# Gate and up products of two SwiGLU layers: from token-major 512-column products to feature-major 256-column products

## The chip, the cores and the metric

The kernel runs on one core of a Trainium2 chip. The metric is the device time of one execution in microseconds. One core holds TensorE (matrix products, PE in the rows, with its weight loads shown apart as PEld), VectorE (DVE), ScalarE (ACT), GpSimd (POOL) and SyncE (SP), which here issues the weight transfers.

## What is computed

Two layers of a streaming encoder on 256 tokens of width 2048. Layer 0 mixes tokens with RWKV-7 heads and state-space heads, layer 1 with chunked attention; each layer ends with a dense SwiGLU block of 5632 hidden features. All of it is in float32. The block is the part that the change touches:

```python
def rms_norm(x, g):
    y = xf * lax.rsqrt(jnp.mean(xf * xf, axis=-1, keepdims=True) + NORM_EPS)
    return (y * g.astype(jnp.float32)).astype(x.dtype)

def swiglu(h, w_gate, w_up, w_down):
    return (jax.nn.silu(h @ w_gate) * (h @ w_up)) @ w_down

for l in range(DEPTH):
    ...                                    # token mixer, sandwich-normed
    h = rms_norm(x, norm_g[l, 2])
    x = x + rms_norm(swiglu(h, ffn_w_gate[l], ffn_w_up[l], ffn_w_down[l]), norm_g[l, 3])
```

## The kernel before, in words

Weights are too large for the core's memory and pass through it once. `stream` (L214) loads two 128-row pieces of a 512-column chunk at a time on SP's queue, and splits each piece into a rounded part `hi` (ScalarE, L230) and the rest `lo` (VectorE, L231), both in the type float32r; five tiles of each are in turn. A product in nearly full float32 precision is then three float32r products: x_hi with w_hi, x_hi with w_lo, x_lo with w_hi. `mm_chunk` (L235) makes them: for each of the nk row pieces and each half of the tokens (t = 0, 1) the activations [128 rows, 128 tokens] are the stationary operand, loaded anew for every product, and 512 weight columns are the moving one (L250, L251, L252). So a row piece takes six products of 512 columns, and the result is token-major: two PSUM tiles of 128 tokens x 512 features. Four PSUM tiles (pool `pmm`) let two chunks overlap.

The row scale of the norm (`rs`, one number per token) is not put on the activations. It is put on the results, where a token is a partition and the scale is one number per partition.

`ffn` (L338) runs for each layer over 11 groups j of 512 hidden features. A group is a gate chunk and an up chunk of 16 row pieces each: 2 x 16 x 6 = 192 products. ScalarE takes SiLU of the scaled gate out of PSUM (L347, two tiles), VectorE multiplies the scaled up result onto it (L350, two tiles). The down product needs hidden features on partitions, so TensorE transposes the group in eight 128 x 128 pieces (L359, into the pool `psa`), and ScalarE and VectorE split what comes out into `hh` (L360) and `hl` (L361). After the eleven groups `out_norm` (L300) runs the down product through `mm_chunk`, squares its result for the second norm (L317), multiplies by the norm's weights (L320 and L328) and adds the residual (L323).

In the built program, TensorE's stream has these transposes a few products into the next group, behind the first row piece's products; VectorE's stream has the two L350 four `lo` tiles into the next chunk.

Of the kernel before, what the change touches and what calls it, by code (L numbers as in the profile page):

```python
# [16 lines left out]
P = 128  # L17
T = 256
# [121 lines left out]
def encoder_body(ctx: ExitStack, tc: tile.TileContext, A):  # L140
# [73 lines left out]
    def stream(wname, n, nk, tail=None):  # L214
        """Yields the k-tiles of column chunk n, split: (hi, lo) tiles [P, 512]; tail: pool of the last four."""
# [19 lines left out]
    def mm_chunk(wname, n, st, width=512, tail=None):  # L235
        """st: list of (hi, lo) tiles [P, 4, T]; returns two PSUM tiles (tokens 0..127, 128..255)."""
# [27 lines left out]
    def split_evac(ps, sh, sl, kts, g):  # L264
        """ps [P, 2, T] (feature-major) times the feature column g(kt), split into hi and lo."""
# [7 lines left out]
    def pre_norm(xt, gname, tag):  # L273
        """xt: 4 token-major tiles [P, 2, 512]. Returns split x*g, feature-major, and its row scale."""
# [25 lines left out]
    def out_norm(ctx2, wname, st, grow, xres, tag, last=False):  # L300
        """x + rms_norm(st @ w) * g; returns 4 token-major tiles."""
# [4 lines left out]
        mg = []  # L306
        for n in range(4):
# [6 lines left out]
            with tc.high_priority(offset=PRI_NORM):  # L314
                for t in range(2):
                    junk = sm.tile([P, 512], mybir.dt.bfloat16, tag="junk", name=f"junk_{tag}_{n}_{t}", bufs=1)
                    act.activation(junk, ps[t], AF.Square, accum_out=ssq[:, t, n:n + 1])  # L317
                    if n == 3:
                        act.activation(rs[:, t:t + 1], ssq[:, t, 3:4], AF.Sqrt, scale=1.0 / D, bias=part[:, t:t + 1])
                        dve.tensor_tensor(m[:, t, :], ps[t], gb, op=ALU.mult)  # L320
# [6 lines left out]
                    else:  # L327
                        dve.tensor_tensor(m[:, t, :], ps[t], gb, op=ALU.mult)  # L328
# [9 lines left out]
    def ffn(l, xt):  # L338
        st, rs = pre_norm(xt, f"g{l}2", f"f{l}")
        with ExitStack() as mx:  # L340
            hp = mx.enter_context(tc.tile_pool(name=f"ff{l}", bufs=2 * NFF, reuse_waits="tile"))
            hid = []
            for j in range(NFF):
                pg = mm_chunk(f"w_gu{l}", 2 * j, st)
                sg = hp.tile([P, 2, 512], F32, tag="sg", name=f"sg_{l}_{j}", bufs=2)
                for t in range(2):
                    act.activation(sg[:, t, :], pg[t], AF.Silu, scale=rs[:, t:t + 1])  # L347
                pu = mm_chunk(f"w_gu{l}", 2 * j + 1, st)
                for t in range(2):
                    dve.scalar_tensor_tensor(sg[:, t, :], pu[t], rs[:, t:t + 1], sg[:, t, :],  # L350
                                             op0=ALU.mult, op1=ALU.mult)
                sh = hp.tile([P, 4, T], F32R, tag="hid", name=f"hh_{l}_{j}")
                sl = hp.tile([P, 4, T], F32R, tag="hid", name=f"hl_{l}_{j}")
                for hh in range(2):
                    ps = psa.tile([P, 2, T], F32, tag="sa", name=f"ht_{l}_{j}_{hh}")
                    for i in range(2):
                        for t in range(2):
                            c0 = (2 * hh + i) * P
                            pe.transpose(ps[:, i, t * P:(t + 1) * P], sg[:, t, c0:c0 + P], ident)  # L359
                    act.copy(sh[:, 2 * hh:2 * hh + 2, :], ps)  # L360
                    dve.tensor_tensor(sl[:, 2 * hh:2 * hh + 2, :], ps, sh[:, 2 * hh:2 * hh + 2, :].bitcast(F32),  # L361
                                      op=ALU.subtract)
                hid.append((sh, sl))
            return out_norm(mx, f"w_dn{l}", hid, 2 * l + 1, xt, f"fo{l}", last=l == 1)

# [561 lines left out]
```

## Time and profile before

| what | us |
|---|---|
| median of 3 runs | 2416.78 (2416.41 to 2418.41) |
| span of the profiled execution, first to last instruction | 2412.1 |
| TensorE busy in it | 2372.9 (98%) |
| weight loads of TensorE busy in it | 1940.9 (80%) |
| VectorE busy | 1424.3 (59%) |
| ScalarE busy | 1267.4 (53%) |
| DMA, mean of the span | 178 GB/s |

The profile was taken in an execution of its own, whose own time is shown only by its span. TensorE's products are pipelined, so the busy time of one (0.39 us) is longer than the distance from one start to the next; the distance is what a product costs in a stream.

### The profile page before, as it was taken

To read this page: it belongs to the slowest core of one execution; us is meant where nothing else is said; L and a number is where in the kernel's file an instruction comes from. 1 tells how busy PE (TensorE), PEld (TensorE's weight loads), DVE (VectorE), ACT (ScalarE), POOL (GpSimd) and SP (SyncE) were. 2 spreads that over 40 slices of the span, in tenths; PEclk is the share of its full clock that TensorE was granted. 3 is DMA by queue.
4 is the path that set the end of the run, shared out by engine and by line. 5 is a ranking of instruction groups with operands and counts; after the bars stand their busy time and mean duration, and the time that the engine had idled before them with its cause. 6 is when DMAs were issued, how large, how long until landed. Compare 5 with 4: busy or idle time off the path is not lost.

```text
span 2412.1 us, 31517 instructions
## 1 busy us (share of the span) xinstructions
PE 2372.9 (98%) x11374; PEld 1940.9 (80%) x11374; DVE 1424.3 (59%) x2340; ACT 1267.4 (53%) x2232; POOL 33.2 (1%) x60
## 2 busy tenths in 40 slices
PE   8999999999999999999999999999999999999998
PEld 7777778878888888888877888887888888888887
DVE  5865967665555555555556555556555555555554
ACT  6646545656445445444446555555544544544443
POOL 0000000000000000000000000000000000000000
PEclk9999999999999999999999999999999999999999
DMA  7433424656666666666675555565666666666665
GB/s 229 142 113 112 140 88 132 190 181 189 192 185 191 192 185 191 192 187 196 196 229 153 180 178 160 172 191 172 189 189 189 190 189 191 189 188 193 199 197 158
DMA packets 119358, 429.17 MB, mean 178 GB/s; under 512 B 13409, under 2 KB 13665, under 8 KB 119201
## 3 DMA queue, kind: packets, MB, share of 16 engines
q1 hardware_dynamic: 115424, 415.46, 56.6%
q0 software_dynamic: 2400, 9.18, 1.5%
q10 hardware_dynamic: 1376, 2.52, 0.3%
q8 instruction: 89, 1.46, 0.3%
q14 instruction: 69, 0.56, 0.1%
HBM read 425.01 MB, written 2.10 MB: 177 GB/s over the span
## 4 chain that ended last, share of the span: by engine, by line
PE 94%; DVE 4%; ACT 1%; issue 1%; DMA 1%; SPq 0%; POOL 0%; DVEq 0%; ACTq 0%; POOLq 0%
PE mm_w_gu L250 13%; PE mm_w_gu L252 13%; PE mm_w_gu L251 13%; PE mm_w_dn L251 7%; PE mm_w_dn L252 7%; PE mm_w_dn L250 7%; PE mm_w_qkv L250 4%; PE mm_w_qkv L251 4%; PE mm_w_qkv L252 4%; PE mm_w_in L252 3%; PE mm_w_in L251 3%; PE mm_w_in L250 3%; PE mm_w_oc L252 1%; PE mm_w_oc L251 1%; PE mm_w_oab L251 1%; PE mm_w_oab L252 1%
## 5 line engine op out<-in xcount | busy, mean ns | idle before, releaser
L231 DVE TENSOR_TENSOR lo_w_gu<-raw_w_gu,hi_w_gu 128x512 fp32r<-128x512 f32 x704 | 486.7, 692 | 433.3 <-ACT hi_w_gu L230 432.4
L230 ACT CAST hi_w_gu<-raw_w_gu 128x512 fp32r<-128x512 f32 x704 | 438.3, 623 | 473.4 <-DVE lo_w_gu L231 424.9
L250 PE MATMUL mm_w_gu<-hi_w_gu,sh_f 128*128 128x512 f32 x1408 | 551.3, 392 | 0.7 <-ACT sh_f L268 0.7
L251 PE MATMUL mm_w_gu<-lo_w_gu,sh_f 128*128 128x512 f32 x1408 | 551.3, 392 | 0.0
L252 PE MATMUL mm_w_gu<-hi_w_gu,sl_f 128*128 128x512 f32 x1408 | 549.2, 390 | 0.0
L231 DVE TENSOR_TENSOR lo_w_dn<-raw_w_dn,hi_w_dn 128x512 fp32r<-128x512 f32 x352 | 242.4, 692 | 218.5 <-ACT hi_w_dn L230 218.2
L230 ACT CAST hi_w_dn<-raw_w_dn 128x512 fp32r<-128x512 f32 x352 | 217.2, 621 | 246.5 <-DVE lo_w_dn L231 233.1
L250 PEld LDWEIGHTS mm_w_gu<-hi_w_gu,sh_f 128*128 128x128 f32 x1408 | 265.1, 188 | 55.6 <-ACT sh_f L268 1.2
L252 PEld LDWEIGHTS mm_w_gu<-hi_w_gu,sl_f 128*128 128x128 f32 x1408 | 265.0, 188 | 54.2
L251 PEld LDWEIGHTS mm_w_gu<-lo_w_gu,sh_f 128*128 128x128 f32 x1408 | 265.2, 188 | 53.2
L251 PE MATMUL mm_w_dn<-lo_w_dn,hh 128*128 128x512 f32 x704 | 276.8, 393 | 0.0
L252 PE MATMUL mm_w_dn<-hi_w_dn,hl 128*128 128x512 f32 x704 | 275.3, 391 | 0.0
L250 PE MATMUL mm_w_dn<-hi_w_dn,hh 128*128 128x512 f32 x704 | 274.8, 390 | 0.0
L231 DVE TENSOR_TENSOR lo_w_qkv<-raw_w_qkv,hi_w_qkv 128x512 fp32r<-128x512 f32 x192 | 132.5, 692 | 102.9 <-ACT hi_w_qkv L230 102.6
L230 ACT CAST hi_w_qkv<-raw_w_qkv 128x512 fp32r<-128x512 f32 x192 | 118.9, 621 | 108.6 <-DVE lo_w_qkv L231 65.5
L231 DVE TENSOR_TENSOR lo_w_in<-raw_w_in,hi_w_in 128x512 fp32r<-128x512 f32 x184 | 125.0, 689 | 56.1 <-ACT hi_w_in L230 54.9
L250 PEld LDWEIGHTS mm_w_dn<-hi_w_dn,hh 128*128 128x128 f32 x704 | 132.1, 188 | 30.1
L250 PE MATMUL mm_w_in<-hi_w_in,sh_in 128*128 128x512 f32 (+1 forms) x384 | 154.5, 402 | 1.4 <-ACT hi_w_in L230 1.4
L252 PE MATMUL mm_w_in<-hi_w_in,sl_in 128*128 128x512 f32 (+1 forms) x384 | 155.2, 404 | 0.0
L251 PEld LDWEIGHTS mm_w_dn<-lo_w_dn,hh 128*128 128x128 f32 x704 | 132.3, 188 | 28.4
L251 PE MATMUL mm_w_qkv<-lo_w_qkv,sh_qkv 128*128 128x512 f32 x384 | 155.1, 404 | 0.0
L252 PEld LDWEIGHTS mm_w_dn<-hi_w_dn,hl 128*128 128x128 f32 x704 | 132.2, 188 | 27.8
(335 smaller groups left out, 2837.5 us busy)
## 6 DMA issues: line engine op xcount, KB each, us to landing
raw_w_gu<-in_w_gu SPq DMA_DIRECT2D x352, 512.0 KB, 3.6
raw_w_dn<-in_w_dn SPq DMA_DIRECT2D x176, 512.0 KB, 4.2
raw_w_qkv<-in_w_qkv SPq DMA_DIRECT2D x96, 512.0 KB, 3.6
raw_w_in<-in_w_in SPq DMA_DIRECT2D x92, 512.0 KB, 3.6
raw_w_oab<-in_w_oab SPq DMA_DIRECT2D x32, 512.0 KB, 3.7
raw_w_oc<-in_w_oc SPq DMA_DIRECT2D x32, 512.0 KB, 4.2
bias<-in_bias POOLq DMA_DIRECT2D x4, 768.0 KB, 7.5
x_in<-in_x SPq DMA_DIRECT2D x4, 512.0 KB, 10.3
```

The lines of the kernel that those rows point to most:

```text
L230: act.copy(hi, raw[:, h, :])
L231: dve.tensor_tensor(lo, raw[:, h, :], hi.bitcast(F32), op=ALU.subtract)
L250: pe.matmul(o, lhsT=xh, rhs=h_[:, :width], start=k_ == 0, stop=False)
L251: pe.matmul(o, lhsT=xh, rhs=l_[:, :width], start=False, stop=False)
L252: pe.matmul(o, lhsT=xl, rhs=h_[:, :width], start=False, stop=k_ == nk - 1)
```

## The change

The gate and up products turn their operands round. A new `mm_feature` loads 128 x 128 pieces of the weights as the stationary operand and moves all 256 tokens past them. Its result has features on partitions and tokens in columns, as the down product wants it, and the eight transposes of a group go. A row piece is now four 128-feature pieces times three products, twelve products of 256 columns, each with its weight load. Since a token is now a column, the row scale of the gate is a multiplication by a tile `rb` that holds the 256 scales in every partition: `token_rows` makes it once per layer, with a product of ones and a diagonal matrix. SiLU then runs in place on the SBUF tile. The up result isn't scaled; its scale moves behind the down product, into `out_norm` (argument `rin`).

```diff
-                pg = mm_chunk(f"w_gu{l}", 2 * j, st)
-                sg = hp.tile([P, 2, 512], F32, tag="sg", name=f"sg_{l}_{j}", bufs=2)
-                for t in range(2):
-                    act.activation(sg[:, t, :], pg[t], AF.Silu, scale=rs[:, t:t + 1])
-                pu = mm_chunk(f"w_gu{l}", 2 * j + 1, st)
-                for t in range(2):
-                    dve.scalar_tensor_tensor(sg[:, t, :], pu[t], rs[:, t:t + 1], sg[:, t, :],
-                                             op0=ALU.mult, op1=ALU.mult)
+                pg = mm_feature(f"w_gu{l}", 2 * j, st)
+                if rb is None:
+                    rb = token_rows(hp, rs, f"f{l}")[:, None, :].broadcast_to([P, 2, T])
+                sg = hp.tile([P, 4, T], F32, tag="sg", name=f"sg_{l}_{j}", bufs=2)
+                for b in range(2):
+                    s2 = sg[:, 2 * b:2 * b + 2, :]
+                    dve.tensor_tensor(s2, pg[b], rb, op=ALU.mult)
+                    act.activation(s2, s2, AF.Silu)
+                pu = mm_feature(f"w_gu{l}", 2 * j + 1, st)
                 sh = hp.tile([P, 4, T], F32R, tag="hid", name=f"hh_{l}_{j}")
                 sl = hp.tile([P, 4, T], F32R, tag="hid", name=f"hl_{l}_{j}")
-                for hh in range(2):
-                    ps = psa.tile([P, 2, T], F32, tag="sa", name=f"ht_{l}_{j}_{hh}")
-                    for i in range(2):
-                        for t in range(2):
-                            c0 = (2 * hh + i) * P
-                            pe.transpose(ps[:, i, t * P:(t + 1) * P], sg[:, t, c0:c0 + P], ident)
-                    act.copy(sh[:, 2 * hh:2 * hh + 2, :], ps)
-                    dve.tensor_tensor(sl[:, 2 * hh:2 * hh + 2, :], ps, sh[:, 2 * hh:2 * hh + 2, :].bitcast(F32),
-                                      op=ALU.subtract)
+                for b in range(2):
+                    f2 = slice(2 * b, 2 * b + 2)
+                    dve.tensor_tensor(sg[:, f2, :], pu[b], sg[:, f2, :], op=ALU.mult)
+                    act.copy(sh[:, f2, :], sg[:, f2, :])
+                    dve.tensor_tensor(sl[:, f2, :], sg[:, f2, :], sh[:, f2, :].bitcast(F32), op=ALU.subtract)
...
+    def mm_feature(wname, n, st):
+        nk = 4 * len(st)
+        ps = [pmm.tile([P, 2, T], F32, tag="mm", name=f"mf_{wname}_{n}_{b}") for b in range(2)]
+        for kt, (hi, lo) in enumerate(stream(wname, n, nk)):
+            sh, sl = st[kt // 4]
+            xh, xl = sh[:, kt % 4, :], sl[:, kt % 4, :]
+            for b in range(2):
+                for i in range(2):
+                    f = slice((2 * b + i) * P, (2 * b + i + 1) * P)
+                    o = ps[b][:, i, :]
+                    pe.matmul(o, lhsT=hi[:, f], rhs=xh, start=kt == 0 and i == 0, stop=False, skip_group_check=True)
+                    pe.matmul(o, lhsT=hi[:, f], rhs=xl, start=False, stop=False, skip_group_check=True)
+                    pe.matmul(o, lhsT=lo[:, f], rhs=xh, start=False, stop=kt == nk - 1, skip_group_check=True)
+        return ps
...
+    def token_rows(pool_, rs, tag):
+        scr = pool_.tile([P, 4, T], F32, tag="sg", name=f"rsd_{tag}", bufs=2)
+        ones = scr[:, 0, 0:P]
+        pool.memset(ones, 1.0)
+        dg = scr[:, 1, :].rearrange("p (t j) -> p t j", t=2)
+        ps = psa.tile([P, 2, P], F32, tag="sa", name=f"rsb_{tag}")
+        for t in range(2):
+            dve.tensor_scalar(dg[:, t, :], ident, rs[:, t:t + 1], None, op0=ALU.mult)
+        pe.matmul(ps, lhsT=ones, rhs=dg, start=True, stop=True)
+        rb = pool_.tile([P, T], F32, tag="rsb", name=f"rb_{tag}", bufs=1)
+        act.copy(rb, ps.rearrange("p a b -> p (a b)"))
+        return rb
...
-                    act.activation(junk, ps[t], AF.Square, accum_out=ssq[:, t, n:n + 1])
+                    ri = 1.0 if rin is None else rin[:, t:t + 1]
+                    act.activation(junk, ps[t], AF.Square, scale=ri, accum_out=ssq[:, t, n:n + 1])
...
-                        dve.tensor_tensor(m[:, t, :], ps[t], gb, op=ALU.mult)
+                        scaled(m[:, t, :], ps[t], ri, gb)
```

`scaled` multiplies by `gb` as before, or, with `rin`, by the row scale and `gb` in one instruction.

TensorE, before, where the second group of layer 0 begins: `mm_w_gu_2_0` and `mm_w_gu_2_1` are the two token halves of that group's gate, `ht` the transposes of the group that has just ended.

```order
L250 MATMUL mm_w_gu_2_0_5323<-hi_w_gu_2_0_0_5327,sh_f_0_4840 128x512
L251 MATMUL mm_w_gu_2_0_5323<-lo_w_gu_2_0_0_5328,sh_f_0_4840 128x512
L252 MATMUL mm_w_gu_2_0_5323<-hi_w_gu_2_0_0_5327,sl_f_0_4841 128x512
L250 MATMUL mm_w_gu_2_1_5324<-hi_w_gu_2_0_0_5327,sh_f_0_4840 128x512
L359 MATMUL ht_0_0_5309<-cc,sg_0_5124 128x128
L359 MATMUL ht_0_1_5316<-cc,sg_0_5124 128x128
L251 MATMUL mm_w_gu_2_1_5324<-lo_w_gu_2_0_0_5328,sh_f_0_4840 128x512
L252 MATMUL mm_w_gu_2_1_5324<-hi_w_gu_2_0_0_5327,sl_f_0_4841 128x512
L359 MATMUL ht_0_0_5309<-cc,sg_0_5124 128x128 x3
L359 MATMUL ht_0_1_5316<-cc,sg_0_5124 128x128 x3
L250 MATMUL mm_w_gu_2_0_5323<-hi_w_gu_2_0_1_5331,sh_f_0_4840 128x512
```

TensorE, after, where the first gate chunk of layer 0 ends and the up chunk begins (the lines are those of the changed file; `mf_w_gu_0_1` holds features 256 to 511 of the gate chunk, `rsb` is the product that spreads the row scale).

```order
L357 MATMUL mf_w_gu_0_1_4947<-sh_f_3_4900,hi_w_gu_0_7_1_5192 128x256
L358 MATMUL mf_w_gu_0_1_4947<-sl_f_3_4901,hi_w_gu_0_7_1_5192 128x256
L359 MATMUL mf_w_gu_0_1_4947<-sh_f_3_4900,lo_w_gu_0_7_1_5193 128x256
L371 MATMUL rsb_f_5222<-rsd_f_5220 128x256
L357 MATMUL mf_w_gu_1_0_5233<-sh_f_0_4840,hi_w_gu_1_0_0_5237 128x256
L358 MATMUL mf_w_gu_1_0_5233<-sl_f_0_4841,hi_w_gu_1_0_0_5237 128x256
L359 MATMUL mf_w_gu_1_0_5233<-sh_f_0_4840,lo_w_gu_1_0_0_5238 128x256
```

Nothing but products of the chunks stands on TensorE between one group and the next now, save one `rsb` in each layer.

VectorE, before, around the end of the second group's up chunk (`mm_w_gu_3`):

```order
L231 TENSOR_TENSOR lo_w_gu_4_1_1_5731<-raw_w_gu_4_1_5724,hi_w_gu_4_1_1_5730 128x512
L350 SCALAR_TENSOR_TENSOR sg_1_5501<-mm_w_gu_3_0_5504,rs_pre,sg_1_5501 128x512
L350 SCALAR_TENSOR_TENSOR sg_1_5501<-mm_w_gu_3_1_5505,rs_pre,sg_1_5501 128x512
L231 TENSOR_TENSOR lo_w_gu_4_2_0_5749<-raw_w_gu_4_2_5746,hi_w_gu_4_2_0_5748 128x512
L231 TENSOR_TENSOR lo_w_gu_4_2_1_5753<-raw_w_gu_4_2_5746,hi_w_gu_4_2_1_5752 128x512
L361 TENSOR_TENSOR hl_1_5685<-ht_1_0_5686,hh_1_5684 128x512
```

VectorE, after, around the end of the second group's gate chunk (`mf_w_gu_2`), where before no VectorE instruction read PSUM:

```order
L231 TENSOR_TENSOR lo_w_gu_3_1_1_5837<-raw_w_gu_3_1_5830,hi_w_gu_3_1_1_5836 128x512
L389 TENSOR_TENSOR sg_1_5789<-mf_w_gu_2_0_5515,rb_f_5226 128x512
L389 TENSOR_TENSOR sg_1_5789<-mf_w_gu_2_1_5516,rb_f_5226 128x512
L231 TENSOR_TENSOR lo_w_gu_3_2_0_5867<-raw_w_gu_3_2_5864,hi_w_gu_3_2_0_5866 128x512
L231 TENSOR_TENSOR lo_w_gu_3_2_1_5871<-raw_w_gu_3_2_5864,hi_w_gu_3_2_1_5870 128x512
```

The two new L389 stand behind the first four `lo` tiles of the next chunk, at the place that L350 has at the end of an up chunk.

## Rows read from the trace of the kernel before

**Rows 1.** The page: busy time by engine, granted clock, chain that ended last.

```profile
PE 2372.9 (98%) x11374; PEld 1940.9 (80%) x11374; DVE 1424.3 (59%) x2340; ACT 1267.4 (53%) x2232; POOL 33.2 (1%) x60
...
PEclk9999999999999999999999999999999999999999
...
PE 94%; DVE 4%; ACT 1%; issue 1%; DMA 1%; SPq 0%; POOL 0%; DVEq 0%; ACTq 0%; POOLq 0%
```

**Rows 2.** Windows, 600 to 1000 us: length, then busy us (and instructions) by engine, clock, DMA.

```profile
600.00:1000.00 400.00, 400.00 (x1799) 329.88 (x1798) 220.99 (x324) 199.33 (x324) 0.00 (x0) 1.00 0.63 189
```

**Rows 3.** Timeline, gate/up stretch: start us, duration us, engine, line, names, shapes.

```profile
899.74 0.39 PE L251 MATMUL mm_w_gu<-lo_w_gu,sh_f 128*128 128x512 f32 x1
899.97 0.39 PE L252 MATMUL mm_w_gu<-hi_w_gu,sl_f 128*128 128x512 f32 x1
899.97 0.19 PEld L250 LDWEIGHTS mm_w_gu<-hi_w_gu,sh_f 128*128 128x128 f32 x1
900.20 0.39 PE L250 MATMUL mm_w_gu<-hi_w_gu,sh_f 128*128 128x512 f32 x1
...
910.62 0.39 PE L251 MATMUL mm_w_gu<-lo_w_gu,sh_f 128*128 128x512 f32 x1
```

**Rows 4.** Timeline, in-projection of layer 0, products of 464 columns, first and last.

```profile
29.79 0.37 PE L250 MATMUL mm_w_in<-hi_w_in,sh_in 128*128 128x464 f32 x1
...
39.60 0.37 PE L252 MATMUL mm_w_in<-hi_w_in,sl_in 128*128 128x464 f32 x1
```

**Rows 5.** Timeline, down product of layer 0, two L250 fifteen products apart.

```profile
1127.82 0.39 PE L250 MATMUL mm_w_dn<-hi_w_dn,hh 128*128 128x512 f32 x1
...
1131.26 0.39 PE L250 MATMUL mm_w_dn<-hi_w_dn,hh 128*128 128x512 f32 x1
```

**Rows 6.** The chain that ended last, in order of time: transposes of consecutive groups.

```profile
667.64 0.66 PE ht L359 x6
712.14 0.66 PE ht L359 x6
756.64 0.66 PE ht L359 x6
```

**Rows 7.** Timeline around the transposes of the first group of layer 0.

```profile
577.74 0.43 PE L359 MATMUL ht<-cc,sg 128*128 128x128 f32 x2
577.90 0.19 PEld L251 LDWEIGHTS mm_w_gu<-lo_w_gu,sh_f 128*128 128x128 f32 x1
...
578.01 0.19 PEld L252 LDWEIGHTS mm_w_gu<-hi_w_gu,sl_f 128*128 128x128 f32 x1
```

**Rows 8.** Timeline, plain float32 products of layer 0 (weight loads, then 256 moving columns).

```profile
354.96 1.86 PEld L789 LDWEIGHTS yd<-xc,L 128*128 128x128 f32 x16
...
210.22 1.89 PE L702 MATMUL g<-sgc,g 128*128 128x256 f32 x8
```

**Rows 9.** Groups by form: count, busy us, mean ns, then idle before and its releaser.

```profile
L231 DVE TENSOR_TENSOR lo_w_gu<-raw_w_gu,hi_w_gu 128x512 fp32r<-128x512 f32 x704 | 486.7, 692 | 433.3 <-ACT hi_w_gu L230 432.4
L350 DVE SCALAR_TENSOR_TENSOR sg<-mm_w_gu,rs_pre,sg 128x512 f32<-128x512 f32 x44 | 30.9, 742 | 0.0
L361 DVE TENSOR_TENSOR hl<-ht,hh 128x512 fp32r<-128x512 f32 x44 | 28.2, 682 | 0.0
L550 DVE TENSOR_TENSOR AA<-aa,cc 128x512 f32<-128x512 f32 x16 | 10.4, 685 | 2.1 <-PE aa L547 2.1
L347 ACT ACTIVATE sg<-mm_w_gu,rs_pre 128x512 f32<-128x512 f32 x44 | 30.2, 687 | 1.2
L360 ACT CAST hh<-ht 128x512 fp32r<-128x512 f32 x44 | 23.5, 585 | 0.0
```

More of the change, by code (lines that the diff above doesn't have):

```diff
@@ L298, in pre_norm, with out_norm @@
         return st, rsqrt_mean(ssum, D, EPS, "pre", [P, 2])
-    def out_norm(ctx2, wname, st, grow, xres, tag, last=False):
+    def out_norm(ctx2, wname, st, grow, xres, tag, last=False, rin=None):
         E = ctx2.enter_context(tc.tile_pool(name="E" + tag, bufs=4, reuse_waits="tile"))
@@ L306, in out_norm, with scaled @@
         mg = []
+        def scaled(out, p_, ri, gb_):
+            if rin is None:
+                dve.tensor_tensor(out, p_, gb_, op=ALU.mult)
+            else:
+                dve.scalar_tensor_tensor(out, p_, ri, gb_, op0=ALU.mult, op1=ALU.mult)
         for n in range(4):
@@ L327, in out_norm @@
                     else:
-                        dve.tensor_tensor(m[:, t, :], ps[t], gb, op=ALU.mult)
+                        scaled(m[:, t, :], ps[t], ri, gb)
                 if n == 0:
@@ L342, in ffn @@
             hid = []
+            rb = None
             for j in range(NFF):
-                pg = mm_chunk(f"w_gu{l}", 2 * j, st)
-                sg = hp.tile([P, 2, 512], F32, tag="sg", name=f"sg_{l}_{j}", bufs=2)
-                for t in range(2):
-                    act.activation(sg[:, t, :], pg[t], AF.Silu, scale=rs[:, t:t + 1])
-                pu = mm_chunk(f"w_gu{l}", 2 * j + 1, st)
-                for t in range(2):
-                    dve.scalar_tensor_tensor(sg[:, t, :], pu[t], rs[:, t:t + 1], sg[:, t, :],
-                                             op0=ALU.mult, op1=ALU.mult)
+                pg = mm_feature(f"w_gu{l}", 2 * j, st)
[7 more added lines that the diff above has]
+                pu = mm_feature(f"w_gu{l}", 2 * j + 1, st)
@@ L363, in ffn @@
                 hid.append((sh, sl))
-            return out_norm(mx, f"w_dn{l}", hid, 2 * l + 1, xt, f"fo{l}", last=l == 1)
+            return out_norm(mx, f"w_dn{l}", hid, 2 * l + 1, xt, f"fo{l}", last=l == 1, rin=rs)
     def mixer0(xt):
```

## The prediction

> **What bounds the kernel now.** I read the page first: TensorE is busy for 98% of the span, the chain that ended last runs through it for 94%, and the granted clock stands in the top tenth throughout [rows 1]. In a stretch that is gate/up work alone, 600 to 1000 us, TensorE is busy for all 400 us at a granted clock of 1.00, the 2.4 GHz level, with VectorE at 221 and ScalarE at 199 us [rows 2]. So in the two SwiGLU blocks the time is the number of products times the distance between them, and nothing else has a say until it takes more than TensorE leaves it. Then the timeline, for the distance: from one L251 at 899.74 to another at 910.62 are 48 products, 10.88 us, **226.7 ns** each [rows 3]. That is not the 0.39 us of a record, which overlaps the next. The weight load of the next product starts with the product before it and has a record of 0.19 us, so at 512 columns it is hidden.
>
> **The products.** Before, a group has 192 products; with 11 groups and two layers that is 4224 x 0.2267 = 957.5 us. After, a row piece has twelve products instead of six, so 8448 products of 256 columns. They move exactly as many columns, and the change breaks even on them if a product of half the width costs half: 113.3 ns. Everything hangs on how much of 226.7 does not shrink with the columns. No float32r product of 256 columns stands in this trace, so I bound it from the widths that do.
>
> Products of 464 columns: 29.79 to 39.60 is 47 of them, 9.81 us, 208.7 ns each [rows 4]. From 464 to 512 columns the distance grows by 18.0 ns for 48 columns, 0.374 ns a column. One column per cycle at 2.4 GHz would be 0.417, or 20.0 ns; the rows lie close to that and on the side of a part that doesn't shrink. Taking one column per cycle (an estimate from these two rows), 512 columns are 213.3 ns and leave 13.3 over; 464 are 193.3 and leave 15.4. The down product, with other tiles in the same form, takes 3.44 us for fifteen, 229.3 ns [rows 5], and leaves 16.0. So each product has some 13 to 16 ns on top of its columns, whatever its width, and the narrower one has no less of it. For 256 columns: 106.7 + 13.3 = 120.0 at the low side, 106.7 + 16.0 = 122.7 at the high side. I take the row that is nearest in width, 15.4: **122 ns**. The products then take 8448 x 0.122 = 1030.7 us, **+73.2 us**.
>
> The outer bounds. Below: the weight load. Sixteen loads of 128 columns stand in 1.86 us, the last of them with its record of 0.19, so 1.67 / 15 = 111 ns from one to the next [rows 8]; two float32r loads behind the transposes start 0.11 us apart [rows 7]. A product can't come faster than its load, so 110 ns is the floor: 8448 x 0.110 - 957.5 = -28 us. Above: the straight line through the 464 and 512 rows, 226.7 - 256 x 0.374 = 131 ns: +149 us. The value of 122 lies between them and is nearest to the two rows of its own kind.
>
> At half the width the load is no longer short beside the product: 111 against 122 ns. It stays hidden only if loads and products overlap wholly. Rows 8 speak for that: there the loads follow at 111 ns although each has a record of 0.19 us, so a load doesn't wait for the one before it to end.
>
> The same rows 8 show plain float32 products of 256 columns: eight in 1.89 us, the last with a record of 0.38, 1.51 / 7 = 216 ns. By the Trainium skill (page "TensorE: Matmul & The Clock Gate", section "Back-to-back issue gap") a warm product comes every N / 2.4 + 2.5 ns, which an estimate puts at 215.8 for 512 columns and 109.2 for 256. By that the products would take 922.5 us, 35 less than now. Rows 3 don't agree: 226.7 at 512 columns, 11 ns more than the rule gives. So I don't take it for the forecast, but the case in which the excess isn't there at 256 columns is a rival below.
>
> **The transposes.** They go, and this is the gain. From one group's transposes to the next are 44.50 us, twice over [rows 6]. The 192 products of a group are 192 x 0.2267 = 43.52. What is left, 0.98 us, is all that a group pays for its eight transposes, the wait for `sg` and the break in the stream: 22 x 0.98 = **-21.5 us**. It is little, since a transpose costs about a tenth of a microsecond and the rest of a group's evictions was beside products already.
>
> **VectorE and ScalarE.** A group gains two L389 on VectorE (128x512 out of PSUM; the nearest row is L550 with 685 ns), and L350 at 742 ns becomes a plain product of two tiles at some 690; L361 keeps its form, from SBUF [rows 9]. That is 44 x 0.69 - 44 x 0.05 = +28 us of VectorE over both layers, about 1.3 us in each 44.5 us group. VectorE has 221 of 400 us taken [rows 2], so it goes from 55 to 58% and the cost is nothing as long as TensorE has split weights in hand. The two L389 wait for the end of a gate chunk with the next `lo` tiles queued behind them, and TensorE waits for those. But four `lo` tiles of the next chunk stand ahead of them, four row pieces of 1.36 us, 5.4 us of TensorE's work against 1.4 us of L389. That is the cover that L350 has now. Were all of it exposed, 44 x 0.69 = 30 us. ScalarE's SiLU and split keep their count and size [rows 9], only their source is SBUF: nothing either way. The scale in `out_norm` rides on instructions that are there already; at the very end one is exposed, of 0.69 us, and takes 0.05 more. `token_rows` puts one plain float32 product of 256 columns, taken at two records of 216 ns [rows 8], into TensorE's stream in each layer: +0.9 us. Its scale is read only at the end of the first gate chunk, when the norm is long done.
>
> **The sum.** 2412.1 + 73.2 - 21.5 + 0.9 = 2464.7 us of span. The span lies 4.7 us under the median of the runs, 2416.8, which I carry over: **2469 us**. The clock stays at 1.00, since TensorE is no less busy than before.
>
> **The rivals.**
> *The fixed part shrinks with the columns (faster).* If 226.7 is 6% on every column, a stall of the stream and not of the product, 256 columns take 113.3 ns, the products break even and the transposes are won: 2412.1 - 21.5 + 0.9 + 4.7 = 2396. For it: the excess at 512 columns is a round sixteenth of 213.3. Against it: 464 columns would take 205.4, and take 208.7. It decides from 115.8 ns down, where the sum crosses the time before. In its sharpest form, with only the load as limit, 110 ns: 2368. By the rule above it would be 109.2 ns, an estimate of 2361.
> *The excess grows as products get shorter.* The load is then in flight all the time and not half of it, and 13.3 becomes 15.4 already at 464 columns. Along that line 131 ns: 2545.
> *A narrow product loses its rate.* The only products of 256 columns here are plain float32 and take 216 ns [rows 8]. If float32r at 256 columns fell to that, or if a product had to wait for the whole 0.23 us from its load's start to its own [rows 3], time per row piece would nearly double: 8448 x 0.216 = 1824.8, some 3263 us. Against it: the loads of rows 8 at 111 ns, and the type, which at 464 columns runs at about one cycle per column.
> *VectorE's cover fails.* +30 us on the forecast, 2499; the four tiles ahead of it speak against it. It lies inside the range and has no chance of its own.
>
> **How the numbers follow.** My forecast, 119 to 125 ns per product (2444 to 2495 us), has 0.53. The growing excess has 0.13, the lost rate 0.07. The shrinking part has 0.16, its sharpest form 0.06. A distance of about 115.8 ns, where gain and loss cancel, has 0.05; "the same" means within 0.2%, 4.8 us, about what a measurement of this kernel can tell from no change. So faster 0.22, same 0.05, slower 0.73. The range goes from 2393, just under the case in which a product costs half, to 2545, the line through the two widths. Outside it stay the sharpest form and the lost rate, together 0.13, and some of the edges.
>
> **What will show it.** The distance between products in a gate/up stretch of the changed kernel: 122 ns, 48 of them in 5.86 us. A group's period, from one L389 to the next group's: 192 x 2 x 0.122 = 46.8 us against 44.50. No transposes, and no gap on TensorE at the end of a chunk. VectorE at about 57% in such a stretch. I am wrong if the distance is 113 or less, or over 131; or if TensorE shows idle time put down to `lo` at the begin of a chunk, which would be VectorE's cover gone; or if it stands at the right distance and the time moves all the same, which would be a stage that I left out.

## The result, and the profile after

The change made the kernel slower by 1.6%. The median of four runs is **2455.7 us** (2453.8 to 2456.9), beside 2417.3 (2416.4 to 2418.4) for the kernel before on the same chip; the ratio is 1.0157, with an interval of 1.0142 to 1.0171. The profiled execution has a span of 2452.0 us, 39.9 more than the 2412.1 of before.

The page of the changed kernel (busy time by engine; granted clock; chain that ended last), to be read against [rows 1]:

```profile
PE 2410.9 (98%) x15426; PEld 2151.3 (88%) x15426; DVE 1445.8 (59%) x2388; ACT 1264.0 (52%) x2234; POOL 33.5 (1%) x62
...
PEclk9999989999999999999999999999999999999999
...
PE 93%; DVE 4%; ACT 1%; issue 1%; DMA 1%; SPq 0%; POOL 0%; DVEq 0%; ACTq 0%; POOLq 0%
```

Nothing has taken TensorE's place: it is busy for 98% as before, with 4052 more instructions (4224 products and two records of each `rb` product come, 176 transposes go). The shares alone don't show that the kernel got slower; the distance between products, from one start to the next, does. The timeline of the changed kernel in a gate/up stretch (start us, duration us, engine, line, names, shapes), the last row 48 products after the first:

```profile
640.14 0.28 PE L357 MATMUL mf_w_gu<-sh_f,hi_w_gu 128*128 128x256 f32 x1
640.26 0.28 PE L358 MATMUL mf_w_gu<-sl_f,hi_w_gu 128*128 128x256 f32 x1
640.38 0.28 PE L359 MATMUL mf_w_gu<-sh_f,lo_w_gu 128*128 128x256 f32 x1
...
645.90 0.28 PE L357 MATMUL mf_w_gu<-sh_f,hi_w_gu 128*128 128x256 f32 x1
```

5.76 us for 48 products are **120.0 ns** each, against 226.7 for twice the columns [rows 3]. Two products of 256 columns take 240.0 ns where one of 512 took 226.7. The records of 0.28 us overlap each other and say nothing of this.

The group's period, in VectorE's part of the timeline (the first `L389` of consecutive groups):

```profile
605.84 1.28 DVE L389 TENSOR_TENSOR sg<-mf_w_gu,rb_f 128x512 f32<-128x512 f32 x2
...
651.92 1.28 DVE L389 TENSOR_TENSOR sg<-mf_w_gu,rb_f 128x512 f32<-128x512 f32 x2
...
698.00 1.28 DVE L389 TENSOR_TENSOR sg<-mf_w_gu,rb_f 128x512 f32<-128x512 f32 x2
```

46.08 us from group to group, twice over, are 384 x 0.120 = 46.08: no break, wait or gap is left in them. Before it was 44.50 [rows 6], of which 43.52 were products. The stretch from 600 to 1000 us, where [rows 2] had 220.99 for VectorE and 199.33 for ScalarE (length; busy us and instructions of PE, PEld, DVE, ACT, POOL; clock; DMA share; GB/s):

```profile
600.00:1000.00 400.00, 400.00 (x3335) 400.00 (x3335) 221.34 (x332) 191.07 (x314) 0.00 (x0) 1.00 0.61 183
```

The weight load (PEld) is now in flight all the time, where it had 329.88 of 400 us, and the clock stays at 1.00, the 2.4 GHz level. The costliest groups by form (as [rows 9]) show who waits for whom:

```profile
L357 PE MATMUL mf_w_gu<-sh_f,hi_w_gu 128*128 128x256 f32 x2816 | 798.5, 284 | 0.7 <-ACT sh_f L268 0.7
L231 DVE TENSOR_TENSOR lo_w_gu<-raw_w_gu,hi_w_gu 128x512 fp32r<-128x512 f32 x704 | 486.2, 691 | 450.6 <-ACT hi_w_gu L230 447.3
L230 ACT CAST hi_w_gu<-raw_w_gu 128x512 fp32r<-128x512 f32 x704 | 435.3, 619 | 515.6 <-PE mf_w_gu L358 480.2
L396 DVE TENSOR_TENSOR sg<-mf_w_gu,sg 128x512 f32<-128x512 f32 x44 | 28.2, 682 | 0.0
```

VectorE waits for ScalarE, ScalarE for TensorE to give a buffer back, and TensorE for next to nothing: 0.7 us of idle before the 2816 products of this line.

**Where the 39.9 us are.** In the chain that ended last, the tail of each `out_norm` begins with its `junk` rows, which cut the program into its stages. Before (start us, duration us):

```profile
521.98 0.70 ACT junk_o L317 x2
...
1261.91 0.70 ACT junk_fo L317 x2
...
1660.93 0.70 ACT junk_o L317 x2
...
2400.98 0.70 ACT junk_fo L317 x2
```

After:

```profile
524.55 0.70 ACT junk_o L325 x2
...
1282.86 0.79 ACT junk_fo L325 x2
...
1682.17 0.70 ACT junk_o L325 x2
...
2440.26 0.79 ACT junk_fo L325 x2
```

The SwiGLU blocks grew from 739.93 to 758.31 and from 740.05 to 758.09 us: +18.4 and +18.0, together **+36.4**. The mixer of layer 1 is the same (399.02 and 399.31), the end after the last row has 0.6 more. The mixer of layer 0, whose code the change leaves alone, has 2.6 more; in the runs below, which leave that stage alone too, the same row stands anywhere from 519 to 527 us, so 2.6 is within its scatter and no effect of the change is shown there.

### The profile page after: what moved, and what is told of

The parts are those of the page before. It is cut to its first block, busy times and chain, and to the rows that moved or that the text cites. A ratio compares the mean times of both kernels' runs of the same rounds, so it can differ in the third digit from the quotient of the medians.

```text
span 2452.0 us, 40069 instructions
## 1 busy us (share of the span) xinstructions
PE 2410.9 (98%) x15426; PEld 2151.3 (88%) x15426; DVE 1445.8 (59%) x2388; ACT 1264.0 (52%) x2234; POOL 33.5 (1%) x62
## 3 DMA queue, kind: packets, MB, share of 16 engines
q10 hardware_dynamic: 1376, 2.52, 0.3%
## 4 chain that ended last, share of the span: by engine, by line
PE 93%; DVE 4%; ACT 1%; issue 1%; DMA 1%; SPq 0%; POOL 0%; DVEq 0%; ACTq 0%; POOLq 0%
PE mf_w_gu L358 14%; PE mf_w_gu L359 14%; PE mf_w_gu L357 14%; PE mm_w_dn L252 7%; PE mm_w_dn L251 7%; PE mm_w_dn L250 6%; PE mm_w_qkv L250 4%; PE mm_w_qkv L252 4%; PE mm_w_qkv L251 4%; PE mm_w_in L252 3%; PE mm_w_in L251 3%; PE mm_w_in L250 3%; PE mm_w_oc L252 1%; PE mm_w_oc L251 1%; PE mm_w_oab L252 1%; PE mm_w_oab L250 1%
## 5 line engine op out<-in xcount | busy, mean ns | idle before, releaser
L357 PE MATMUL mf_w_gu<-sh_f,hi_w_gu 128*128 128x256 f32 x2816 | 798.5, 284 | 0.7 <-ACT sh_f L268 0.7
L358 PE MATMUL mf_w_gu<-sl_f,hi_w_gu 128*128 128x256 f32 x2816 | 798.4, 284 | 0.2 <-DVE sl_f L269 0.2
L359 PE MATMUL mf_w_gu<-sh_f,lo_w_gu 128*128 128x256 f32 x2816 | 798.2, 283 | 0.0
L357 PEld LDWEIGHTS mf_w_gu<-sh_f,hi_w_gu 128*128 128x128 f32 x2816 | 541.2, 192 | 1.2 <-ACT sh_f L268 1.2
L358 PEld LDWEIGHTS mf_w_gu<-sl_f,hi_w_gu 128*128 128x128 f32 x2816 | 541.6, 192 | 0.7 <-DVE sl_f L269 0.6
L359 PEld LDWEIGHTS mf_w_gu<-sh_f,lo_w_gu 128*128 128x128 f32 x2816 | 541.7, 192 | 0.0
L250 PE MATMUL mm_w_dn<-hi_w_dn,hh 128*128 128x512 f32 x704 | 273.2, 388 | 0.0
L250 PEld LDWEIGHTS mm_w_dn<-hi_w_dn,hh 128*128 128x128 f32 x704 | 132.2, 188 | 29.5
L250 PE MATMUL mm_w_in<-hi_w_in,sh_in 128*128 128x512 f32 (+1 forms) x384 | 154.8, 403 | 1.5 <-ACT hi_w_in L230 1.5
## 6 DMA issues: line engine op xcount, KB each, us to landing
x_in<-in_x SPq DMA_DIRECT2D x4, 512.0 KB, 11.1
```

The lines of the kernel that those rows point to most:

```text
L250: pe.matmul(o, lhsT=xh, rhs=h_[:, :width], start=k_ == 0, stop=False)
L357: pe.matmul(o, lhsT=hi[:, f], rhs=xh, start=kt == 0 and i == 0, stop=False, skip_group_check=True)
L358: pe.matmul(o, lhsT=hi[:, f], rhs=xl, start=False, stop=False, skip_group_check=True)
L359: pe.matmul(o, lhsT=lo[:, f], rhs=xh, start=False, stop=kt == nk - 1, skip_group_check=True)
```

## The experiments

The distance per product has to explain nearly everything, so most runs are about it. Those that shorten products write part of each result only, from the second row piece of a chunk on. Their totals are worth nothing; their distances are read chunk by chunk from the timeline, and where a chunk has transposes in its stream, from the chunk beside it.

### Widths with feature-stationary weights

`mm_feature` gets another width for each group of layer 0, and other stationary sizes, an order by terms and equal operands in layer 1:

```diff
+    WIDTHS = (256, 240, 224, 208, 192, 160, 128, 64, 256, 256, 256)
+    KINDS = ("as", "byterm", "m96", "m64", "m32", "same", "as", "as", "as", "as", "as")
...
-                    pe.matmul(o, lhsT=hi[:, f], rhs=xl, start=False, stop=False, skip_group_check=True)
+                    pe.matmul(o, lhsT=hi[:, f], rhs=x2[:, :c], start=False, stop=False, skip_group_check=True)
```

> The changed kernel; in the first SwiGLU layer the moving tokens of all row pieces but the first are cut, group by group, from 256 to 240, 224, 208, 192, 160, 128, 64 (three last groups 256 again); in the second layer groups keep 256 columns but vary: three terms in turn over the four feature pieces instead of piece by piece, stationary pieces of 96, 64, 32 columns, one stationary and one moving operand for all three products. Output is not the reference's where columns are left out or operands swapped. Theory A, columns at 2.4 GHz plus 13.3 ns, with a floor of 110 ns set by the weight load: 240 columns 113.3, 224 and below 110. Theory B, 120 ns is the floor of a load and not columns plus a fixed part: 120 at every width from 256 down. Theory C, the straight line through 256 (120.0) and 512 (226.7) has a fixed part that the load takes from the stream, in proportion to its stationary columns: 96 columns 116.7, 64 columns 113.3, 32 columns 110.0 ns at 256 moving columns; by A with a part that belongs to the product itself all three stay at 120. Order of the terms and equal operands: A and C expect 120, unless the fixed part comes from writing the same PSUM columns three times in a row, which would show in the order by terms.

Measured, mean distance in a chunk: 120.0 ns at 256 columns, 112.0 at 240, then 111.6, 111.6, 111.6, 111.5 and 111.4 at 224, 208, 192, 160 and 128. Two widths in the timeline, each with 21 products from its first row to its last, 2.35 and 2.34 us:

```profile
603.86 0.28 PE L373 MATMUL mf_w_gu<-sh_f,hi_w_gu 128*128 128x240 f32 x1
...
606.21 0.27 PE L373 MATMUL mf_w_gu<-sh_f,hi_w_gu 128*128 128x240 f32 x1
...
800.06 0.27 PE L373 MATMUL mf_w_gu<-sh_f,hi_w_gu 128*128 128x128 f32 x1
...
802.40 0.27 PE L373 MATMUL mf_w_gu<-sh_f,hi_w_gu 128*128 128x128 f32 x1
```

Almost half the columns go and the time stands still: from 224 columns down each product waits for something that doesn't depend on its columns, at 111.4 ns, which is what the loads of [rows 8] had. The 120.0 at 256 columns is not that floor but stands 8.6 ns above it. So the theory that 120 is a limit of the load falls. At 240 columns theory A had 113.3, so there the part over the columns is 12.0 and not 13.3. Order by terms and equal operands leave 120.0 as it is. Fewer stationary columns lower it a little: 116.0 with 96, 113.4 with 64 and 113.5 to 117.8 with 32. A share of the load in the distance fits the first two and not the third. So at 256 columns the load is not shown to be wholly out of the distance.

At 64 columns the distance began at 111 to 112 ns and then went to 213. The windows of that kernel, of which 128-column products fill the first, 64-column products nearly all of the second, and 256-column products the last (columns as above; the third lies inside the second):

```profile
800.00:840.00 40.00, 40.00 (x358) 40.00 (x358) 23.21 (x35) 19.39 (x33) 0.00 (x0) 1.00 0.66 198
840.00:880.00 40.00, 40.00 (x230) 40.00 (x228) 15.71 (x25) 14.07 (x24) 0.00 (x0) 0.62 0.43 129
847.00:877.00 30.00, 30.00 (x143) 30.00 (x142) 9.34 (x15) 8.46 (x14) 0.00 (x0) 0.50 0.39 117
920.00:960.00 40.00, 40.00 (x336) 40.00 (x335) 20.97 (x33) 18.80 (x31) 0.00 (x0) 1.00 0.61 184
```

The granted clock is at its 1.2 GHz level (0.50) for the whole of 847 to 877 us, while PE and PEld are busy without a break; more under the last heading. A row piece of 256-column products stands in that stretch, and in the kernel before two products of 512 columns stand in a short stretch at the same level, behind the break at the end of the first SwiGLU block:

```profile
873.93 0.41 PE L375 MATMUL mf_w_gu<-sh_f,lo_w_gu 128*128 128x256 f32 x1
...
875.85 0.41 PE L375 MATMUL mf_w_gu<-sh_f,lo_w_gu 128*128 128x256 f32 x1
...
1271.31 0.63 PE L251 MATMUL mm_w_qkv<-lo_w_qkv,sh_qkv 128*128 128x512 f32 x1
1271.74 0.63 PE L250 MATMUL mm_w_qkv<-hi_w_qkv,sh_qkv 128*128 128x512 f32 x1
```

Nine products of 256 columns take 1.92 us, 213.3 ns each, and those of 512 are 0.43 us apart (427 ns in the trace). Both are one column per cycle of 1.2 GHz with nothing over, so the 13.3 ns show at the 2.4 GHz level only. (The 64-column products of that stretch are 213 ns apart as well, so the floor that was 111 to 112 ns has doubled.)

### Widths and tokens in the order of before

The same ladder in `mm_chunk` of the kernel before: tokens stand still, weights move, so the number of columns changes without the change's orientation.

```diff
+    WIDTHS = (512, 480, 448, 416, 384, 320, 256, 192, 512, 512, 512)
+    TOKENS = (128, 96, 64, 32, 128, 128, 128, 128, 128, 128, 128)
...
+                        o = ps[t][:m, :c]
+                        pe.matmul(o, lhsT=xh, rhs=h_[:, :c], start=k_ == 0, stop=False, skip_group_check=True)
```

> The kernel before; in the first SwiGLU layer the moving weight columns of all row pieces but the first are cut, group by group, to 480, 448, 416, 384, 320, 256, 192 (first and last three groups 512); in the second layer the stationary tokens of groups 1 to 3 are cut to 96, 64 and 32 at 512 moving columns. Output is not the reference's, since columns or tokens are left out. Theory A, columns at 2.4 GHz plus 13.3 ns: 213.3, 200.0, 186.7, 173.3, 146.7, 120.0 and, at 192, the load's floor of 110 ns; so at 256 columns the same 120.0 as the changed kernel, whichever operand stands still. Rival, the line through 464 and 512 columns of the trace before: 256 columns 131 ns, 384 columns 179 ns. Rival, the feed of split weights is what paces the kernel before (ScalarE 0.62 and VectorE 0.69 us one after the other make 1.36 us, as long as six products of 226.7): then no width below 512 is faster, and row pieces stay at 1.36 us. Stationary tokens: if the load takes its part from the stream in proportion, 223.3, 220.0, 216.7 ns at 96, 64, 32; if the part belongs to the product, 226.7 throughout.

Measured: 217 ns at 480 columns, 207 at 448, 187 at 416, 173.4 at 384, 146.6 at 320, 120 at 256 (the median; the mean is 127 to 143, because these products are faster than the split weights come) and 111 at 192. From the timeline, twelve products of 384 columns in 2.08 us, 15 of 320 in 2.20 and 21 of 256 in 2.52:

```profile
717.10 0.33 PE L256 MATMUL mm_w_gu<-hi_w_gu,sh_f 128*128 128x384 f32 x1
...
719.18 0.33 PE L256 MATMUL mm_w_gu<-hi_w_gu,sh_f 128*128 128x384 f32 x1
...
747.91 0.31 PE L256 MATMUL mm_w_gu<-hi_w_gu,sh_f 128*128 128x320 f32 x1
...
750.11 0.31 PE L256 MATMUL mm_w_gu<-hi_w_gu,sh_f 128*128 128x320 f32 x1
...
764.32 0.28 PE L256 MATMUL mm_w_gu<-hi_w_gu,sh_f 128*128 128x256 f32 x1
...
766.84 0.28 PE L256 MATMUL mm_w_gu<-hi_w_gu,sh_f 128*128 128x256 f32 x1
```

From 256 to 384 columns the distance grows by 53.4 ns for 128 columns, 0.417 a column, which is one column per cycle of 2.4 GHz. At that rate 384, 320 and 256 columns are 160.0, 133.3 and 106.7, and each leaves **13.3 ns**, as 512 columns do. The widths between don't: 480 leave 17 ns, 448 leave 20, 416 some 13 to 15. The line through 464 and 512 would have been 179 at 384. And at 256 columns it is 120 whichever operand stands still: width and number of products are what costs, the orientation as such costs nothing that shows here. Fewer tokens at 512 columns gave no less: 230 ns with 96 and 64, 232 with 32.

### What the 13.3 ns hang on

A grid of widths and stationary tokens, again in `mm_chunk` of before:

```diff
+    GRID = (((128, 512), (128, 384), (96, 384), (64, 384), (32, 384), (128, 320), (64, 320), (32, 320), (128, 512),
+             (64, 512), (128, 512)),
+            ((128, 512), (128, 496), (128, 464), (128, 432), (128, 400), (128, 368), (128, 352), (128, 336),
+             (128, 304), (128, 288), (128, 512)))
```

> The kernel before; after the first row piece of a chunk, groups of the first SwiGLU layer use fewer stationary tokens and moving columns: (tokens, columns) = (128, 384), (96, 384), (64, 384), (32, 384), (128, 320), (64, 320), (32, 320), then (64, 512); in the second layer 128 tokens with 496, 464, 432, 400, 368, 352, 336, 304, 288 columns. Output is not the reference's, since tokens or columns are left out. So far 256, 320 and 384 moving columns left 13.3 ns over their columns and 416 to 480 left 13 to 20; at 256 moving columns 64 stationary ones left 6.7, at 512 they left 17. Theory A, the part comes from the weight load in proportion to its stationary columns where nothing else disturbs: 173.3, 170.0, 166.7, 163.3 ns at 384, and 146.7, 140.0, 136.7 at 320. Theory D, the part belongs to how a product and the load beside it fall into step, and no simple share of either: then no such series, and widths that are not multiples of 64 scatter between 10 and 20 ns over their columns. Second layer by a constant 13.3: 220.0, 206.7, 193.3, 180.0, 166.7, 160.0, 153.3, 140.0, 133.3.

Measured: at 384 columns 173.4 ns with 128, 96, 64 or 32 tokens, at 320 columns 146.6 with 128 and 64 and 143 to 147 with 32. So at these widths the part isn't proportional to the stationary columns; that theory falls, and the drop at 256 columns with fewer of them stays unexplained. Over its columns a product takes 13.3 ns at 496 and 368, 13.4 at 336, 13.7 at 400, 14.4 at 352, but 15.8 at 432, **16.6 at 464**, 11.1 at 304 and some 12 at 288. Sixty-four tokens at 384 columns, twelve products in 2.08 us; then three neighbours of 464, whose starts stand 0.22 and 0.20 us apart in turn:

```profile
672.75 0.33 PE L257 MATMUL mm_w_gu<-hi_w_gu,sh_f 128*64 128x384 f32 x1
...
674.83 0.33 PE L257 MATMUL mm_w_gu<-hi_w_gu,sh_f 128*64 128x384 f32 x1
...
1710.21 0.38 PE L257 MATMUL mm_w_gu<-hi_w_gu,sh_f 128*128 128x464 f32 x1
1710.43 0.37 PE L258 MATMUL mm_w_gu<-lo_w_gu,sh_f 128*128 128x464 f32 x1
1710.63 0.38 PE L259 MATMUL mm_w_gu<-hi_w_gu,sl_f 128*128 128x464 f32 x1
```

The excess of 464 columns is no step of a trend towards narrow products. It belongs to a band: from 432 to 480 columns 16 to 20 ns are left over, with 13.3 at 496 on one side of it and 13.7 at 400 on the other. So a constant 13.3 holds at 256, 320, 336, 368, 384, 496 and 512 columns, and not at every width.

### The transposes alone

The kernel before, with the transposes left out and `sg` read as it stands:

```diff
-                    ps = psa.tile([P, 2, T], F32, tag="sa", name=f"ht_{l}_{j}_{hh}")
-                    for i in range(2):
-                        for t in range(2):
-                            c0 = (2 * hh + i) * P
-                            pe.transpose(ps[:, i, t * P:(t + 1) * P], sg[:, t, c0:c0 + P], ident)
+                    ps = sg[:, hh, :].rearrange("p (a t) -> p a t", a=2)
```

> The kernel before without the eight transposes of a group; the split reads the token-major tile in SBUF as if it were the transposed one, so the down product gets features and tokens in the wrong places. My sum put 0.98 us on a group for transposes, wait and break: group period 43.52 instead of 44.50 us, 22 x 0.98 = 21.5 us less, 2396 us. If only the transposes' own distance counts, 176 x 0.109 = 19.2 us, 2398. If they were hidden, no change, 2417.

Measured: 2394.0 us, a ratio of 0.991 (0.9895 to 0.9925) to the 2414.5 of before on that chip, 20.6 us less. Its chain:

```profile
526.34 0.70 ACT junk_o L317 x2
...
1255.59 0.70 ACT junk_fo L317 x2
...
1653.08 0.70 ACT junk_o L317 x2
...
2382.28 0.70 ACT junk_fo L317 x2
```

The SwiGLU blocks take 729.25 and 729.20 us, 10.68 and 10.85 less than before: 21.5 together. This is what the change could win at most, and the term of the sum to the tenth. The group's period shows it without the scatter of the stages: from one group's first SiLU to the next are 43.52 us, the 192 products and nothing else, where it was 44.50.

```profile
646.05 0.69 ACT L347 ACTIVATE sg<-mm_w_gu,rs_pre 128x512 f32<-128x512 f32 x1
...
689.57 0.69 ACT L347 ACTIVATE sg<-mm_w_gu,rs_pre 128x512 f32<-128x512 f32 x1
```

### The change in one layer

```diff
+                if l == 0:
+                    pg = mm_feature(f"w_gu{l}", 2 * j, st)
...
+                else:
+                    pg = mm_chunk(f"w_gu{l}", 2 * j, st)
...
+            return out_norm(mx, f"w_dn{l}", hid, 2 * l + 1, xt, f"fo{l}", last=l == 1, rin=rs if l == 0 else None)
```

> The change in the first SwiGLU layer alone; the second is as before, with its transposes. By my sum the change costs 704 / 2 x 2 x 0.080 us in products less 11 x 0.98 us in transposes per layer, half of the whole: some 18 us, so 2414.5 + 18 = 2433 us beside 2414.5 for the kernel before. If something outside the two blocks took the difference (the start, the mixers, code loading), the half would cost clearly more or less than 18.

Measured: 2436.1 us, ratio 1.0081 (1.0066 to 1.0096) to 2416.6: +19.4, half of the change's loss. Its chain puts 758.28 us into the first SwiGLU block and 738.44 into the second, so the layer with the change pays as it does in the whole change, and the one without it stands 1.6 us under the kernel before:

```profile
526.96 0.70 ACT junk_o L325 x2
...
1285.24 0.79 ACT junk_fo L325 x2
...
1686.17 0.70 ACT junk_o L325 x2
...
2424.61 0.70 ACT junk_fo L325 x2
```

### VectorE's cover

The changed kernel with each `L389` done three times:

```diff
-                    dve.tensor_tensor(s2, pg[b], rb, op=ALU.mult)
+                    for _ in range(3):
+                        dve.tensor_tensor(s2, pg[b], rb, op=ALU.mult)
```

> The changed kernel, with the two multiplications of the gate by the row scale (L389 of the changed kernel) made three times over, four more VectorE instructions of 0.685 us at the end of every gate chunk; they read the same PSUM and write the same tile with the same values. My sum put VectorE's part of the change at nothing, because four tiles of split weights stand ahead: then 2456 as the changed kernel, and the product distance stays at 120.0 ns. If VectorE's evictions were on the path, 88 x 0.685 = 60 us more, 2516.

Measured: 2455.2 us (2453.0 to 2456.1), ratio 1.0161 (1.0146 to 1.0177) to before: the changed kernel's own time. In its gate/up stretch VectorE has 20 us more, and TensorE the same 3335 products:

```profile
600.00:1000.00 400.00, 400.00 (x3335) 400.00 (x3335) 241.48 (x366) 191.58 (x313) 0.00 (x0) 1.00 0.60 183
```

Three times the scaling ahead of the `lo` tiles costs nothing, so once costs nothing either.

### Fewer products in the new orientation

If the number of products is the cost, eight for a row piece instead of twelve should win some back. `x_hi` and `x_lo` are laid side by side, one product of 512 columns takes both against `hi`, one of 256 takes `x_hi` against `lo`, and VectorE adds the halves:

```diff
-                    pe.matmul(o, lhsT=hi[:, f], rhs=xh, start=kt == 0 and i == 0, stop=False, skip_group_check=True)
-                    pe.matmul(o, lhsT=hi[:, f], rhs=xl, start=False, stop=False, skip_group_check=True)
-                    pe.matmul(o, lhsT=lo[:, f], rhs=xh, start=False, stop=kt == nk - 1, skip_group_check=True)
+                pe.matmul(ps[q], lhsT=hi[:, f], rhs=w2, start=kt == 0, stop=kt == nk - 1, skip_group_check=True)
+                pe.matmul(ps[q][:, 0, :], lhsT=lo[:, f], rhs=w2[:, 0, :], start=False, stop=kt == nk - 1,
+                          skip_group_check=True)
```

> The changed kernel, with x_hi and x_lo side by side, so that a piece of w_hi meets both in one product of 512 columns and a piece of w_lo meets x_hi in one of 256: eight products for a row piece instead of twelve, on the same 3072 columns. The two halves of a result are added by VectorE when they leave PSUM. Theory A (13.3 ns for every product): a row piece takes 3072 / 2.4 + 8 x 13.3 = 1387 ns against 1440, a group 44.4 against 46.1 us, 704 x 0.0533 = 37.5 us less than the changed kernel, 2418 us, level with the kernel before. If the fixed part grew with the columns and not with the products, nothing would change, 2456. VectorE gets eight instructions of some 0.7 us more in each group; were they exposed, up to 121 us on top, 2539.

Measured: 2427.8 us, ratio 1.0066 (1.0039 to 1.0093) to 2414.5. It wins back more than half of the loss, which speaks for the count of products as its cause, but it is 10 us over what was expected. A wide and a narrow product together take 351 ns on average instead of 226.7 + 120.0 = 346.7, the wide ones 230 to 241. Most of the excess is in the first layer, where a pair takes 354 ns; in the second, with the same shapes, it takes 348. The next kernel has the four wide ones of a row piece in a row, then the four narrow ones, in case the turn from one to the other costs it:

```diff
-                pe.matmul(ps[q], lhsT=hi[:, f], rhs=w2, start=kt == 0, stop=kt == nk - 1, skip_group_check=True)
...
+            for q in range(4):
+                pe.matmul(ps[q], lhsT=hi[:, q * P:(q + 1) * P], rhs=w2, start=kt == 0, stop=kt == nk - 1,
+                          skip_group_check=True)
+            for q in range(4):
+                pe.matmul(ps[q][:, 0, :], lhsT=lo[:, q * P:(q + 1) * P], rhs=w2[:, 0, :], start=False,
+                          stop=kt == nk - 1, skip_group_check=True)
```

> As the run with eight products for a row piece, with the order changed: first the four products of 512 columns, then the four of 256, instead of in turn. In turn they took 347 to 361 ns for a pair (230 to 240 for the wide, 114 to 120 for the narrow one), where 226.7 + 120.0 = 346.7 was expected. If the excess comes of the two widths in turn, sorted products return to 226.7 and 120.0, 1387 ns a row piece, and the time to 2418 less what the other chip runs faster, some 2415; if it is in the wide product itself, or in its operands, it stays at about 2428.

Measured: 2427.0 us, ratio 1.005 (1.0033 to 1.0067). The order of the widths isn't it. Its timeline, where a row of four has its products' common time:

```profile
700.73 1.09 PE L365 MATMUL mf_w_gu<-sl_f,hi_w_gu 128*128 128x512 f32 x4
701.65 0.64 PE L368 MATMUL mf_w_gu<-sl_f,lo_w_gu 128*128 128x256 f32 x4
702.13 1.09 PE L365 MATMUL mf_w_gu<-sl_f,hi_w_gu 128*128 128x512 f32 x4
```

A row piece takes 702.13 - 700.73 = 1.40 us, between the 1.44 of the changed kernel and the 1.36 of before. The wide four take 0.92 us from their start to that of the narrow ones, 230 ns each where 226.7 stands in [rows 3]. Neither of the two beats the kernel before.

## Why the prediction was right

**The bound** was TensorE alone, and is. The sum was one of products and transposes, and both of these terms have runs of their own. The third, 0.9 us for `rsb`, shows in the trace: its product holds the stream up by 0.43 us in each layer.

**The products' distance** carried everything. The step was right in kind: a part of about 13 ns per product that doesn't shrink with the columns, so that the 4224 additional products pay 4224 x 13.3 ns, about 56 us, for moving the same columns. It was mis-sized by 2 ns: I took the excess of the 464 column row, 15.4, because that row was nearest in width, over the 13.3 of the very same operands at 512. The measured 120.0 is the low side that stood beside it. 8448 x 0.002 = **16.9 us** is the whole miss of that term. The widths show why: 464 lies in the band from 432 to 480 columns whose excess is larger. The down product's 16.0 misled in the same direction. The premise behind the term, 13 to 16 ns on every product "whatever its width", was too strong: 448 columns have 20 and 304 have 11. That 256 columns have the 13.3 of 512 again could not be read from the two rows, and that the forecast came as near as 2 ns is in part luck.

**The transposes**, -21.5, were measured alone at -21.5 between stages and -20.6 in the medians, and a group's period fell by 0.98 us. The period that was read from the chain, less the products in it, was a good price: it held the break in the stream and not only the instructions.

**The sum with 120.0**: the products are 8448 x 0.120 - 957.5 = +56.3 us, and +56.3 - 21.5 + 0.9 = +35.7; the two blocks show +36.4. The rest of the 39.9 is the 2.6 of layer 0's mixer, 0.3 and 0.6 elsewhere. The span lies 3.7 us under the median, not the 4.7 that I carried over. From the forecast: 2469 - 16.9 + 0.7 + 2.6 + 0.9 - 1.0 = 2455.3, within a microsecond of the median.

**The rival in which the fixed part shrinks** (113.3 ns, 2396 us) is out: 13.3 ns stand at 512, 384, 320 and 256 columns alike. Its sharpest form had the rule of the Trainium skill beside it (page "TensorE: Matmul & The Clock Gate", section "Back-to-back issue gap": N / 2.4 + 2.5 ns), which the page gives as the gap of an isolated product and not for a stream of loads and products, a limit that the prediction left out. By that rule 256 columns would be 109.2 ns, an estimate; the trace has 120.0, and at each of these widths about 10.8 more than the rule gives. **The rival in which the excess grows** (131) is out by the same widths: it does grow from 512 to 448 columns, and is gone again at 384. **A narrow float32r product that loses its rate** (216) is out by all of them.

**The load's floor** was taken as 110 ns and is 111.4. That the load doesn't set the distance at 256 columns was right, and closer than it looked: at 240 the distance is within a nanosecond of the floor. That it is wholly hidden there is not shown, since 64 stationary columns in place of 128 bring 120.0 down to 113.4. From 224 columns down to 64 a product at the 2.4 GHz level costs 111 to 112 ns, however many of them it moves.

**VectorE's cover** held, with room for at least two more passes. VectorE's share I had at 57 to 58% and it is 55%: a group has more work in a longer period, and `L396`, which stands for the old `L350`, got cheaper as forecast, 682 ns against 742.

**The clock** stayed at 1.00 as forecast, but the reason given for it, that TensorE is no less busy, doesn't carry: with 64 columns TensorE and its loads were busy for all of 847 to 877 us, and the granted clock was 0.50.

**What stays open** is what the 13.3 ns are. At 320 and 384 columns they aren't the load in proportion to its columns; at 256 they aren't the order of the terms or the operands, but may be in part the load; the turn between widths isn't what made the kernels with eight products slower than expected. They show at the 2.4 GHz level only, and other widths have 11 to 20 ns. That each product costs about so much over its columns is measured; why it does is not.

## What to carry to other kernels

Where a stream of products is bound by TensorE and each has its own weight load, count the products before the columns: here, at the 2.4 GHz level, each costs its columns at one per cycle plus 13.3 ns, so going from 512 columns to 256 costs 13.3 ns for every product that it adds. Other widths have 11 to 20 ns. Removing transposes from such a stream is worth their break, 0.98 us for eight, and has to be weighed against that. Take the fixed part from the row with the same operands, and look for a second width before reading a trend into one that differs.

## What the runs showed of the hardware

- In streams of one width, float32r products with a load of 128 stationary columns each came 111.4 to 111.6 ns apart on average, from 224 columns down to 128. At 240 it was 112.0, at 256 it was 120.0.
- In the stretch with products of 64 columns at that distance the granted clock went from 1.00 to 0.50, the 1.2 GHz level (0.50 from 847 to 877 us, 0.62 on the mean of 840 to 880), although TensorE and its loads were busy for all of it, and the distance went from 112 to 213 ns. In the window with 128 columns at the same distance it was 1.00, and it was 1.00 again in the window with 256 columns.
- At that lower level the part over the columns is gone: 213.3 ns at 256 columns and 427 at 512, where the 2.4 GHz level has 120.0 and 226.7. A product of 256 columns so costs 1.78 times as much at half the clock, not twice.
- The distance at 512 columns isn't one number: 226.7 ns for gate/up, 229.3 for the down product [rows 5], 230 with 64 or 96 tokens, 224 to 241 for the wide products of the kernels with eight, and there 237 on the mean of one layer and 231 in the other, with the same shapes. Nothing tried here shows what chooses it.
